# All 22 hidden chunks of the FFNs' up projection in seven products, opened by the two products that need only the first token half

## The chip, the cores and the metric

The kernel runs on one core of a Trainium2 chip. The metric is the device time of one execution in microseconds (us); before is the kernel as it was, after is the kernel with the change. One execution of each is also recorded by the hardware profiler, and the views below are of that record. PE is TensorE, DVE is VectorE, ACT is ScalarE, POOL is GpSimd and SP is SyncE, which only issues loads here.

## What is computed

A trunk of two layers on 768 tokens (a prompt of 512 and a sample of 256, which share the weights). Each layer is a macaron block:

```
x = x + 0.5 * swiglu_ffn(rmsnorm(x, norm_g[li, 0]), ffn_w1[li, 0], ffn_w2[li, 0])
x = x + mixer(rmsnorm(x, norm_g[li, 1]))        # layer 0: HGRN2, layer 1: windowed attention
x = x + 0.5 * swiglu_ffn(rmsnorm(x, norm_g[li, 2]), ffn_w1[li, 1], ffn_w2[li, 1])

def swiglu_ffn(x, w1, w2):
    gate, up = jnp.split(x @ w1, 2, axis=-1)
    return (jax.nn.silu(gate) * up) @ w2
```

The width is 1024 and the FFN's hidden width is 2816, all in fp32. There are four FFNs: f0, then HGRN2, f1 and f2 one behind the other, then the attention, f3.

## The kernel before

**Numbers.** Every fp32 factor is split into a high part (a cast on ACT) and a low part (a subtraction on DVE or, for one weight block in seven, on POOL), and each product is three matmuls: high by high, high by low, low by high. An operand is ready when both parts are: the split of a token tile is L266 (ACT) and L267 (DVE), that of a weight L199 and L200, or L166 and L167 for a weight that is staged whole.

**Chunks and halves.** The hidden width is 22 chunks of 128; chunk i has 128 gate columns and 128 up columns of w1. The tokens are two halves of 384 (three blocks of 128 each), the model width two parts of 512. The normed and transposed input of an FFN thus has four tiles, b00 and b10 (first half of tokens, parts 0 and 1) and b01 and b11 (second half). Each tile has four slices of 128, held in two pairs `kp`.

**Plain and in seven products.** Chunks 0 and 1 are multiplied plainly (`up_plain`): for each token half, gate and up are 8 slices x 3 matmuls of 128x384 each, so 96 matmuls for a chunk and 192 for the two. Chunks 2 to 21 go by `up_pair`, a Strassen-Winograd scheme over (gate, up) x (token half) with seven products p1 to p7 of 12 matmuls each, 84 for a chunk. A product takes one combination of weight blocks, which is staged, and one factor of the tokens:

```
FACTOR = {"p1": "b00", "p2": "b10", "p3": "b11", "p4": "t4", "p5": "t1", "p6": "t2", "p7": "t3"}
```

The sums t1 to t4 combine the four tiles. `sums` and `mix` make them once for an FFN, on DVE (L350, L351, L353, L354), each followed by a split (a cast on ACT, L266, and a subtraction on DVE, L267), for each of two halves kp of a part. `product` issues the 12 matmuls of a product (L421). The hidden values of four chunks (a group) go through `down_quad`, also in seven products (L479), with `add_x` adding the results to x (L501).

**Weights.** SP loads raw columns into four buffers `wr` and, for the chunks in seven products, one more block into `s3`. POOL's accumulating DMAs (L141) add a11 to the block in s3 and a22 to a21, in place. DVE adds a11 += a21 (L206) and a12 += a11 (L210) between the splits. `quad_steps` lists the staging of one chunk's seven weights in the order UP; `plain_steps` stages a whole 128-column block. Staging runs ahead of use as far as eight staged buffers `w` allow.

**Order.** The code is written in program order, and a scheduler places each instruction in the queue of its engine; each engine works through its queue in order and waits by semaphores. What is to be mixed into the opening of an FFN (the transposes of the second token half, the sums) is put on a list of deferred steps, which `run_later` takes from. Before an FFN the residual additions of the stage ahead end block by block, and each block of 128 tokens is normed at once (`norm_block`: L303 and L304 on ACT, L305 and L306 on DVE), transposed on PE (L323), scaled on its way out of PSUM by ACT (L326), and split.

## Time and profile before

| what | value |
|---|---|
| time, median of 3 runs | 2863.37 us (2861.89 to 2866.12) |
| time of the profiled execution | 2862.54 us |
| its span, first to last instruction | 2860.7 us |
| mean granted clock of TensorE | 0.995 |
| busy share of PE, DVE, ACT, POOL | 98%, 77%, 46%, 11% |
| first matmul of the opening of f1, and of its down projection | 1070.57 us, 1136.32 us |
| first matmul of the down projection of f2, of f3 | 1635.36 us, 2422.50 us |

Rows in order of time give the start from the beginning of the span, how long the row was busy, engine, source line and operation, the program's names for the output and inputs, the shapes, the number of instructions that the row holds, and in square brackets how long the engine was idle before it and what released it. L261, L262 and L263 are the three matmuls of a plain product, L421 those in the seven products. In the page's groups the numbers behind the shapes are total busy us, mean ns of one, and idle time ahead with its releaser. A matmul's duration contains waiting in a pipeline; the distance from one start to the next is what it costs.

### The profile page before, as it was taken

To read this page: it belongs to the slowest core of one execution; us is meant where nothing else is said; L and a number is where in the kernel's file an instruction comes from. 1 tells how busy PE (TensorE), PEld (TensorE's weight loads), DVE (VectorE), ACT (ScalarE), POOL (GpSimd) and SP (SyncE) were. 2 spreads that over 40 slices of the span, in tenths; PEclk is the share of its full clock that TensorE was granted. 3 is DMA by queue.
4 is the path that set the end of the run, shared out by engine and by line. 5 is a ranking of instruction groups with operands and counts; after the bars stand their busy time and mean duration, and the time that the engine had idled before them with its cause. 6 is when DMAs were issued, how large, how long until landed. Compare 5 with 4: busy or idle time off the path is not lost. (4 is left out here: it accounts for less than half of the span.)

```text
span 2860.7 us, 40520 instructions
## 1 busy us (share of the span) xinstructions
PE 2802.9 (98%) x15225; PEld 2559.9 (89%) x15225; DVE 2195.0 (77%) x3846; ACT 1318.2 (46%) x2454; POOL 303.9 (11%) x306
## 2 busy tenths in 40 slices
PE   8999999999999999999999999999999899999998
PEld 8899999889899889998998999989887779989897
DVE  7788787477577658778878878887859978778877
ACT  7344443434344435433444543444457755434443
POOL 1111111000000001111111111111000001111110
PEclk9999999999999999999999999999999999999999
DMA  6555454311111133554544355544412113554442
GB/s 165 128 122 124 120 133 118 111 45 38 45 41 34 64 92 89 133 132 119 122 118 107 92 137 129 124 118 120 131 54 74 45 37 91 134 129 123 118 122 96
DMA packets 330101, 291.37 MB, mean 102 GB/s; under 512 B 11608, under 2 KB 257840, under 8 KB 329904
## 3 DMA queue, kind: packets, MB, share of 16 engines
q1 hardware_dynamic: 294064, 212.43, 25.0%
q0 software_dynamic: 31680, 62.93, 12.7%
q10 hardware_dynamic: 4160, 13.42, 1.3%
q8 instruction: 119, 1.95, 0.3%
q14 instruction: 78, 0.64, 0.1%
HBM read 216.39 MB, written 9.44 MB: 79 GB/s over the span
## 5 line engine op out<-in xcount | busy, mean ns | idle before, releaser
L421 PE MATMUL ps<-big,w 128*128 128x384 f32 x6720 | 1172.6, 334 | 3.3 <-DVE tA L444 2.9
L421 PEld LDWEIGHTS ps<-big,w 128*128 128x128 f32 x6720 | 1165.6, 188 | 8.6 <-DVE tA L444 6.9
L199 ACT CAST w<-wr 128x512 fp32r<-128x512 f32 x600 | 416.1, 707 | 724.6 <-PE ps L421 328.3
L479 PE MATMUL ps<-w,big 128*128 128x512 f32 x2520 | 586.8, 391 | 15.8 <-DVE x L501 15.6
L479 PEld LDWEIGHTS ps<-w,big 128*128 128x128 f32 x2520 | 469.6, 188 | 127.9 <-DVE x L501 16.7
L200 DVE TENSOR_TENSOR w<-wr,w 128x512 fp32r<-128x512 f32 (+1 forms) x520 | 437.0, 850 | 95.4 <-ACT w L199 86.5
L501 DVE SCALAR_TENSOR_TENSOR x<-ps,x 128x512 f32<-128x512 f32 x468 | 305.5, 682 | 21.5 <-PE ps L479 11.1
L141 POOL DMA_DIRECT2D s<-wr x120 | 105.6, 880 | 1620.4 <-DMA wr<-in_ffn_w_dram 611.5
L261 PE MATMUL ps<-w,big 128*128 128x512 f32 x624 | 249.5, 400 | 0.2
L263 PE MATMUL ps<-w,big 128*128 128x512 f32 x624 | 245.5, 394 | 2.0 <-DVE big L330 1.4
L262 PE MATMUL ps<-w,big 128*128 128x512 f32 x624 | 244.8, 392 | 0.0
L266 ACT CAST big<-tA 128x384 fp32r<-128x384 f32 x296 | 147.9, 512 | 171.2 <-DVE tA L449 70.4
L261 PE MATMUL ps<-big,w 128*128 128x384 f32 (+2 forms) x640 | 221.0, 347 | 3.4 <-ACT big L266 2.0
L262 PE MATMUL ps<-big,w 128*128 128x384 f32 (+2 forms) x640 | 217.1, 339 | 0.7 <-DVE big L267 0.4
L263 PE MATMUL ps<-big,w 128*128 128x384 f32 (+2 forms) x640 | 215.7, 337 | 0.0
L167 DVE TENSOR_TENSOR w<-wr,w 128x1024 fp32r<-128x1024 f32 x92 | 111.3, 1220 | 81.7 <-ACT w L166 57.6
L267 DVE TENSOR_TENSOR big<-tA,big 128x384 fp32r<-128x384 f32 x296 | 164.1, 565 | 8.4 <-ACT big L266 5.1
L206 DVE TENSOR_TENSOR wr<-wr,wr 128x512 f32<-128x512 f32 (+1 forms) x100 | 79.3, 793 | 113.4 <-DMA wr<-wr 84.6
L141 POOL DMA_DIRECT2D wr<-wr x100 | 87.2, 872 | 678.2 <-DVE tA L350 332.6
L166 ACT CAST w<-wr 128x1024 fp32r<-128x1024 f32 x92 | 96.6, 1052 | 121.7 <-PE ps L262 100.5
L263 PEld LDWEIGHTS ps<-w,big 128*128 128x128 f32 x624 | 117.6, 188 | 28.1 <-DVE big L330 2.1
L261 PEld LDWEIGHTS ps<-w,big 128*128 128x128 f32 x624 | 118.0, 189 | 22.5 <-ACT w L166 0.3
(170 smaller groups left out, 3298.6 us busy)
## 6 DMA issues: line engine op xcount, KB each, us to landing
wr<-in_ffn_w_dram SPq DMA_DIRECT2D x264, 512.0 KB, 3.8
s<-in_ffn_w_dram SPq DMA_DIRECT2D x120, 256.0 KB, 3.0
s<-wr POOLq DMA_DIRECT2D x120, 256.0 KB, 3.8
wr<-wr POOLq DMA_DIRECT2D x80, 256.0 KB, 3.8
wr<-in_hg_w_in_dram SPq DMA_DIRECT2D x40, 512.0 KB, 3.7
wr<-wr POOLq DMA_DIRECT2D x20, 512.0 KB, 4.6
spill<-x ACTq DMA_DIRECT2D x12, 512.0 KB, 3.2
x<-spill ACTq DMA_DIRECT2D x12, 512.0 KB, 3.2
```

Of the source, the lines that this page charges most:

```text
L141: self.nc.gpsimd.dma_start(out, src, accum_op=ALU.add)
L167: self.nc.vector.tensor_sub(lo, raw, hi.bitcast(F32))
L199: nc.scalar.copy(h, src)
L200: (eng or nc.vector).tensor_sub(l, src, h.bitcast(F32))
L261: nc.tensor.matmul(out, a[0], b[0], start=first, stop=False)
L262: nc.tensor.matmul(out, a[0], b[1], start=False, stop=False)
L263: nc.tensor.matmul(out, a[1], b[0], start=False, stop=last)
L266: self.nc.scalar.copy(hi, src)
L267: self.nc.vector.tensor_sub(lo, src, hi.bitcast(F32))
L421: self.nc.tensor.matmul(ps, a[x], b[y], start=first and k == 0 and i == 0, stop=k == 3 and i == 2, skip_group_check=True,)
L479: nc.tensor.matmul(ps, a[x], w[y], start=name == chain and kp == 0 and q == 0, stop=kp == 1 and q == 2, skip_group_check=True,)
L501: self.nc.vector.scalar_tensor_tensor(x, ps, c, x, ALU.mult, ALU.add)
```

## The change

`up_plain` and PLAIN are gone, and all 22 chunks are planned in seven products. In the first group of an FFN `open_pairs` runs ahead: for chunks 0 and 1, then for 2 and 3, the products p1 (with b00) and p2 (with b10), both of which have gate columns as weight, 96 matmuls in all. Their weights are the two halves of the gate columns, which are staged whole by the plain step; so the gate columns of these four chunks are loaded twice, once there and once for the rest. `up_pair` then does the other five products of these chunks, in the order REST. `quad_steps` does a11 += a21 after p7 and a12 += a11 after p4 in that order. `mix` puts t3 ahead of t1, and the b01 tile, which no product uses by itself, is no longer split.

```
-PLAIN = 2
-GROUPS = (NF - PLAIN) // 4
+GROUPS = NF // 4
+REST = ("p7", "p5", "p4", "p6", "p3")
...
-        def p1():
-            split("p1", [a11])
-            nc.vector.tensor_add(a11, a11, a21)
-
-        def p2():
-            split("p2", [a12])
-            nc.vector.tensor_add(a12, a12, a11)
...
+        own = {"p1": [a11], "p2": [a12], "p3": [a12], "p4": [a22], "p5": [a21], "p6": [a11], "p7": s3}
+        second = lambda: nc.vector.tensor_add(a11, a11, a21)
+        fourth = lambda: nc.vector.tensor_add(a12, a12, a11)
+        after = {"p7": second, "p4": fourth} if order == REST else {"p1": second, "p2": fourth}
...
             for kp in range(2):
-                self.put(f"b{part}{half}", kp, self.tn[(part, half)][:, kp])
+                if part or not half:
+                    self.put(f"b{part}{half}", kp, self.tn[(part, half)][:, kp])
...
         sub(b22, b12, b22)
         sub(b12, b11, b12)
+        put("t3", b22)
         put("t1", b12)
         sub(b11, b11, b22)
         sub(b21, b21, b11)
         put("t4", b21)
-        put("t3", b22)
         put("t2", b11)
...
+            self.plan_quad((tag, i), (gate, up), (NC, P), REST if i < 4 else UP)
+
+        for i in range(4):
+            self.plan((tag, i, "gate"), w1[:, i * P : (i + 1) * P], (NC, P))
...
+    def open_pairs(self, tag, js):
+        opened = {j: (self.ps(H), self.tmp(H)) for j in js}
+        for part in range(2):
+            for j, (a, v) in opened.items():
+                key = (tag, j, "gate")
+                w = tuple(t[:, 4 * part : 4 * part + 4, :] for t in self.take(key))
+                self.multiply(a, w, FACTOR["p2" if part else "p1"], not part, part)
+                if part:
+                    self.done(key)
+                    self.nc.scalar.activation(a, a, AF.Silu)
+                else:
+                    self.nc.scalar.copy(v, a)
+                if part or js[0] or len(self.deferred) > 3:
+                    self.run_later()
+        return opened
...
             if g == 0:
-                ts = {}
-                for half in range(2):
-                    for j in range(PLAIN):
-                        t = ts[2 * j + half] = self.up_plain(tag, j, half)
-                        name = f"b{j}{half}"
-                        if name != "b01":
-                            put(name, t, 0)
-                gather(ts, 0)
+                for i in range(0, 4, 2):
+                    opened.update(self.open_pairs(tag, (i, i + 1)))
                 self.run_later(len(self.deferred))
```

Line numbers shift with it: L398 of after is a matmul of any product (before L421), L259 and L260 the split of a token tile (before L266 and L267), L205 and L206 the additions a11 += a21 and a12 += a11 (before L206 and L210), L474 a matmul of the down projection (before L479).

How the instructions stand now is shown at three places of f1's opening. Names in front of the underscore are the program's tiles. First PE, behind the matmuls that need only the first token half. Before, the second half of the two plain chunks follows, on the split b01 tile (big_1284):

```order
3676 L261 MATMUL ps_1304_9214<-big_1276_9044,w_1263_9001 128x384
3677 L262 MATMUL ps_1304_9214<-big_1276_9044,w_1263_9001 128x384
3678 L263 MATMUL ps_1304_9214<-big_1276_9044,w_1264_9002 128x384
3679 L261 MATMUL ps_1307_9245<-big_1284_9103,w_1231_8834 128x384
3680 L262 MATMUL ps_1307_9245<-big_1284_9103,w_1231_8834 128x384
```

After, at the end of the opening products (big_1288 is a part of b10), come products on the sums: big_1313 and big_1317 are the two halves of t3, big_1314 and big_1318 those of t1, big_1316 one of t2:

```order
3542 L398 MATMUL ps_1311_9191<-big_1288_9068,w_1276_9026 128x384
3543 L398 MATMUL ps_1329_9300<-big_1313_9208,w_1293_9113 128x384 x6
3544 L398 MATMUL ps_1330_9301<-big_1314_9211,w_1294_9117 128x384 x6
3545 L398 MATMUL ps_1328_9299<-big_1316_9219,w_1301_9158 128x384
3546 L398 MATMUL ps_1343_9402<-big_1313_9208,w_1325_9274 128x384 x2
3547 L398 MATMUL ps_1329_9300<-big_1317_9224,w_1293_9113 128x384
3548 L398 MATMUL ps_1330_9301<-big_1318_9227,w_1294_9117 128x384
```

So the products that use the sums have moved up to directly behind the work on the first token half.

Second ACT, between b10 and the casts of b11 (before: big_1280 is b01, big_1287 is b11):

```order
790 L326 ACTIVATE big_1280_9086<-ps_1279_9082,cols_92 128x384
791 L326 ACTIVATE big_1280_9086<-ps_1281_9088,cols_92 128x384
792 L326 ACTIVATE big_1280_9086<-ps_1282_9093,cols_92 128x384
793 L326 ACTIVATE big_1280_9086<-ps_1283_9098,cols_92 128x384
794 L266 CAST big_1284_9103<-big_1280_9086 128x2x384
795 L266 CAST big_1285_9106<-big_1280_9086 128x2x384
796 L326 ACTIVATE big_1287_9125<-ps_1286_9121,cols_92 128x384
797 L326 ACTIVATE big_1287_9125<-ps_1288_9127,cols_92 128x384
798 L326 ACTIVATE big_1287_9125<-ps_1289_9132,cols_92 128x384
799 L326 ACTIVATE big_1287_9125<-ps_1290_9137,cols_92 128x384
800 L266 CAST big_1291_9142<-big_1287_9125 128x2x384
801 L266 CAST big_1292_9145<-big_1287_9125 128x2x384
```

After (big_1296 is b01, big_1303 is b11; two copies L418 stand ahead of b01's four):

```order
801 L319 ACTIVATE big_1296_9125<-ps_1299_9137,cols_92 128x384
802 L199 CAST w_1293_9113<-s3_1249_8876 128x512
803 L199 CAST w_1294_9117<-wr_1248_8874 128x512
804 L416 ACT_TABLE_LOAD
805 L416 ACTIVATE ps_1289_9071<-ps_1289_9071 128x384
806 L199 CAST w_1300_9154<-wr_1248_8874 128x512
807 L199 CAST w_1301_9158<-wr_1247_8872 128x512
808 L416 ACTIVATE ps_1291_9073<-ps_1291_9073 128x384
809 L319 ACTIVATE big_1303_9166<-ps_1302_9162,cols_92 128x384
810 L319 ACTIVATE big_1303_9166<-ps_1304_9168,cols_92 128x384
811 L319 ACTIVATE big_1303_9166<-ps_1305_9173,cols_92 128x384
```

The b01 casts are gone, and four staging casts, a table load and two Silus stand between b01 and b11.

Third DVE, at the residual additions ahead of f1's opening (x_1193 before and x_1205 after are token block 2). Before:

```order
1155 L499 TENSOR_TENSOR x_1193_8537<-ps_1244_8897,x_1193_8537 128x512
1156 L305 RECIPROCAL stat_1246_8912<-stat_1246_8912 128x1
1157 L306 TENSOR_SCALAR big_1245_8911<-x_1193_8537,stat_1246_8912 128x1024
1158 L499 TENSOR_TENSOR x_1194_8539<-ps_1247_8917,x_1194_8539 128x512
1159 L465 TENSOR_TENSOR x_1191_8533<-x_1191_8533,x_1194_8539 128x512
```

After, wr_1247 and wr_1248 being the raw gate and up columns of chunk 0:

```order
1172 L494 TENSOR_TENSOR x_1205_8561<-ps_1256_8921,x_1205_8561 128x512
1173 L205 TENSOR_TENSOR wr_1247_8872<-wr_1247_8872,wr_1248_8874 128x512
1174 L206 TENSOR_TENSOR wr_1247_8872<-wr_1247_8872 128x512
1175 L298 RECIPROCAL stat_1258_8936<-stat_1258_8936 128x1
1176 L299 TENSOR_SCALAR big_1257_8935<-x_1205_8561,stat_1258_8936 128x1024
1177 L494 TENSOR_TENSOR x_1206_8563<-ps_1259_8941,x_1206_8563 128x512
```

The two additions of the weight staging now stand between block 2's residual addition and its norm. In f2 the first of them stands behind block 1's residual additions.

More of the change, by code (lines that the diff above doesn't have):

```diff
@@ L396, in plan_ffn, with multiply @@
             self.plan((tag, "last", c), w2[(NF - 2) * P :, c * 512 : (c + 1) * 512], (2, 512))
-    def up_plain(self, tag, j, half):
-        pss = []
-        for c in range(2):
-            wh, wl = self.take((tag, j, c))
-            ps = self.ps(H)
-            for k in range(NC):
-                b = self.operand(f"b{k // 4}{half}", k % 4)
-                self.mm3(ps, (wh[:, k, :], wl[:, k, :]), b, k == 0, k == NC - 1)
-                if half == 0 and k in (((), (2, 6)), ((3, 7), (3, 7)))[j][c]:
-                    self.run_later()
-            if half:
-                self.done((tag, j, c))
-            pss.append(ps)
-        t = self.tmp(H)
-        self.nc.scalar.activation(t, pss[0], AF.Silu)
-        self.nc.vector.tensor_mul(t, t, pss[1])
-        return t
     def product(self, key, name, src, ps, first, last):
-        wh, wl = self.take((*key, name))
+        self.multiply(ps, self.take((*key, name)), src, first, last)
+        self.done((*key, name))
+    def multiply(self, ps, w, src, first, last):
         for k in range(4):
-            a, b = (wh[:, k, :], wl[:, k, :]), self.operand(src, k)
+            a, b = (w[0][:, k, :], w[1][:, k, :]), self.operand(src, k)
             for i, (x, y) in enumerate(((0, 0), (0, 1), (1, 0))):
```

44 lines of the change are left out of this document (18 added, 26 removed).

## The prediction

> **What bounds the kernel now.** I read the page's busy times first, then TensorE (PE) in order of time at one opening of an FFN, and there the queues of ScalarE (ACT), VectorE (DVE) and GpSimd (POOL). The second FFN (f1) stands for the others.
>
> ```profile
> PE 2802.9 (98%) x15225; PEld 2559.9 (89%) x15225; DVE 2195.0 (77%) x3846; ACT 1318.2 (46%) x2454; POOL 303.9 (11%) x306
> ```
>
> PE is busy for 98% of the span, so a removed matmul is worth its pitch if its successors are ready. Any new wait of PE is paid in full.
>
> ```profile
> 1070.57 0.60 PE L261 MATMUL ps<-big,w 128*128 128x384 f32 x2
> ...
> 1084.66 0.33 PE L263 MATMUL ps<-big,w 128*128 128x384 f32 x1
> ...
> 1089.00 0.33 PE L261 MATMUL ps<-big,w 128*128 128x384 f32 x1
> ...
> 1107.20 1.03 PE L421 MATMUL ps<-big,w 128*128 128x384 f32 x5
> ...
> 1136.32 2.01 PE L479 MATMUL ps<-w,big 128*128 128x512 f32 x8
> ```
>
> These are f1's first plain matmul (1070.57), two rows 25 matmuls apart, the first matmul of a product (1107.20) and the first of the down projection (1136.32). The pitch is 4.34 / 25 = 0.1736 us. The 192 plain matmuls take 33.33 of the 36.63 us before 1107.20; the other 3.30 are transposes of the second half and short waits.
>
> **Matmuls removed.** Four chunks cost 2 x 96 + 2 x 84 = 360 matmuls before and 4 x 84 = 336 after. That is 24 x 0.1736 = 4.17 us for an FFN, 16.7 for four, and the whole gain; the built program's order has these 96 fewer on PE.
>
> **The cover that goes with them.** Before, 192 matmuls need no sum of token halves; after, only the 96 of the two opening products do not. PE ends those at 1070.57 + 16.67 + 3.30 = 1090.54. Next in its queue stand 60 matmuls (10.42 us) that use all eight sum operands (t3, t1, t4, t2, two halves each). When are these ready?
>
> ```profile
> 1075.72 1.59 ACT L266 CAST big<-big 128x768 fp32r<-128x768 f32 x2
> 1077.18 2.03 ACT L326 ACTIVATE big<-ps,cols 128x384 f32<-128x384 f32 x4
> 1079.04 1.62 ACT L266 CAST big<-big 128x768 fp32r<-128x768 f32 x2
> 1080.50 2.11 ACT L326 ACTIVATE big<-ps,cols 128x384 f32<-128x384 f32 x4
> 1082.50 1.56 ACT L266 CAST big<-big 128x768 fp32r<-128x768 f32 x2
> 1084.09 1.28 ACT L412 ACT_TABLE_LOAD   x1
> ```
>
> ```profile
> 1083.37 1.83 DVE L267 TENSOR_TENSOR big<-big,big 128x768 fp32r<-128x768 f32 x2 [1.58 <-ACT big L266]
> 1085.11 0.95 DVE L350 TENSOR_TENSOR big<-big,big 128x768 f32<-128x768 f32 x1
> ...
> 1089.74 0.95 DVE L354 TENSOR_TENSOR big<-big,big 128x768 f32<-128x768 f32 x1
> 1090.61 0.95 DVE L350 TENSOR_TENSOR big<-big,big 128x768 f32<-128x768 f32 x1
> ...
> 1095.41 0.68 DVE L200 TENSOR_TENSOR w<-wr,w 128x512 fp32r<-128x512 f32 x1
> 1096.02 0.95 DVE L353 TENSOR_TENSOR big<-big,big 128x768 f32<-128x768 f32 x1
> ...
> 1099.83 2.69 DVE L267 TENSOR_TENSOR big<-big,big 128x768 fp32r<-128x768 f32 x3
> ```
>
> ```profile
> 1070.00:1085.00 15.00, 14.91 (x96) 14.27 (x95) 11.83 (x15) 14.98 (x26) 1.73 (x2) 1.00 0.44 105
> 1085.00:1100.00 15.00, 15.00 (x88) 15.00 (x88) 14.88 (x21) 8.37 (x14) 0.00 (x0) 1.00 0.01 2
> 1107.00:1136.00 29.00, 29.00 (x170) 29.00 (x169) 22.22 (x34) 14.37 (x25) 3.97 (x4) 1.00 0.50 119
> ```
>
> ACT turns out b10, b01 and b11 without a gap, and DVE's chain of sums starts when b11 is split. The table of stretches (columns PE, weight loads, DVE, ACT, POOL, clock, share of the DMA engines, GB/s) says that ACT is the limit up to 1085 (14.98 of 15) and DVE after it (14.88 of 15). Before, the last operand is out at 1099.83 + 3 x 0.87 = 1102.4, 4.8 us ahead of PE. The change takes 16.67 us of cover from that. What it does to the chain is priced from these rows:
>
> ```profile
> L199 ACT CAST w<-wr 128x512 fp32r<-128x512 f32 x480 | 289.7, 620 | 565.3 <-PE ps L421 254.2 <-PE ps L479 251.0 <-issue 38.5
> L442 ACT ACTIVATE ps<-ps 128x384 f32<-128x384 f32 x80 | 37.9, 474 | 14.5 <-PE ps L421 14.5
> L438 ACT COPY tA<-ps 128x384 f32<-128x384 f32 x80 | 37.9, 473 | 3.0 <-PE ps L421 1.3
> L206 DVE TENSOR_TENSOR wr<-wr,wr 128x512 f32<-128x512 f32 x80 | 54.8, 685 | 0.6
> L210 DVE TENSOR_TENSOR wr<-wr 128x512 f32<-128x512 f32 x80 | 56.7, 709 | 1.2
> 1102.59 2.15 POOL L200 TENSOR_TENSOR w<-wr,w 128x512 fp32r<-128x512 f32 x1 [21.05 <-ACT w L199]
> 1103.97 1.32 DVE L210 TENSOR_TENSOR wr<-wr 128x512 f32<-128x512 f32 x1
> ```
>
> ACT, between the casts of b10 and those of b11: the b01 casts go (1080.50 - 1079.04 = 1.46). Two copies (0.95), four staging casts (4 x 0.62 = 2.48), the table load (1.28) and two Silus (0.95) come, 5.66 in duration. Neighbours overlap by about 0.1 us each, so 4.9, and net +3.4. The load moves from behind the b11 casts to ahead of them. The first sum then starts at 1085.11 + 3.4 = 1088.5.
>
> DVE: eight sums and eight splits of a pitch of 0.87 (1090.61 - 1089.74), 13.9 us, and four staging subtractions among them at 0.61 (1096.02 - 1095.41), 2.4 us. The last operand is out at 1104.8. The plain product's L413 and its split, which stood among the sums before, are gone; the b01 split went from an idle stretch and gives nothing. A staging subtraction of POOL also falls into the chain; beside such a one the a12 addition took 1.32 us instead of 0.71, so +0.6 at most here. Six matmuls (1.04) follow the last operand, so PE ends the 60 at 1105.9 to 1106.5 instead of 1090.54 + 10.42 = 1100.96. I take a wait of 5.0 us, the end without POOL's delay; bounds 4.0 (a third of ACT's additions lie in gaps) and 5.6.
>
> The Trainium skill ("SBUF — State Buffer", section "SBUF: two separate sides") calls the port pair of DVE and GpSimd an exclusive lock, for which the loser waits out the whole instruction. By it the added delay could be as long as POOL's 2.15 us, and the total 1.5 us higher for each FFN than by the 0.6 of the row; the measured row decides.
>
> The rest of the opening is PE's: 180 matmuls, 31.2 us or 15 products. From 1107 to 1136 DVE spent 22.22 us on 14 products, so 15 need some 24 of 31. POOL and SP each issue 24 instructions more, since chunks 0 to 3 load their gate twice; DMA shares of 0.44, 0.01 and 0.50 hide that, for nothing.
>
> **A new wait ahead of the opening.** DVE's queue of after has quad 0's a11 addition right behind the residual addition of token block 2. It waits for POOL's accumulating DMA. Queued behind it are that block's norm and the second half's additions; ACT, PE's transposes and so the first matmul wait for these.
>
> ```profile
> 1060.40 0.68 DVE L499 TENSOR_TENSOR x<-ps,x 128x512 f32<-128x512 f32 x1
> 1062.63 0.16 DVE L305 RECIPROCAL stat<-stat 128x1 f32<-128x1 f32 x1 [1.55 <-ACT stat L304]
> ...
> 1060.19 0.88 POOL L141 DMA_DIRECT2D wr<-wr  x1 [2.29 <-DVE stat L305]
> ...
> wr<-wr POOLq DMA_DIRECT2D x1, 256.0 KB, 3.3
> ...
> 1555.31 1.88 DVE L501 SCALAR_TENSOR_TENSOR x<-ps,x 128x512 f32<-128x512 f32 x3
> 1558.32 0.69 DVE L501 SCALAR_TENSOR_TENSOR x<-ps,x 128x512 f32<-128x512 f32 x1 [1.13 <-PE ps L263]
> ...
> 1557.83 0.86 POOL L141 DMA_DIRECT2D wr<-wr  x1 [4.61 <-DVE x L501]
> ```
>
> In f1 the DMA is issued at 1060.19 and lands 3.3 later, 1063.5. The addition and the next one (0.6 each at their pitch) put the norm at 1064.7 instead of 1062.63: 2.1 us late, of which I take 1.8, as PE has a little other work. Bounds are 0 (issued early enough) and 2.1. In f2 it stands behind block 1's additions, which end at 1557.2, and the DMA lands at 1561.1: 4.0 late, taken as 3.4 since down matmuls remain; bounds 1.0 and 4.5. The fourth FFN follows a projection as f1 does: 1.8. The first has no additions ahead of it: 0.
>
> **Sum**, against the profiled execution (2862.54, span 2860.7): f0 -4.17 + 5.0 = +0.8; f1 -4.17 + 5.0 + 1.8 = +2.6; f2 -4.17 + 5.0 + 3.4 = +4.2; f3 +2.6. Together +10.2, so 2872.7; the median of the runs (2863.37) is 0.83 above this execution, which gives 2873.6.
>
> **The rivals.** *The operands come in time, faster.* Place: the second halves of t4 and t2. Price: up to 16.7 us. It decides where the last operand is out by 1100, that is 5 us earlier than I count. ACT's 8.37 busy of 15 after 1085 and its casts that wait for staging slots rather than for work speak for it; DVE's 14.88 of 15 speaks against it. With the early waits small too the time is 2847 to 2857, about 2852.
>
> *Waits eat just the saving.* With 4.0 us of wait and half the early shifts (0, 0.9, 1.7, 0.9) the sum is -0.7 + 3.5 = +2.8, 2866; with none, 2863. Measurement of this kernel tells from no change about 0.2%, 5.7 us, so this is 2857.6 to 2869.1.
>
> *The clock falls, much slower.* The sums' waits could halve the clock:
>
> ```profile
> 2313.68 0.50 PE L1157 MATMUL ps<-tA,big 128*128 128x512 f32 x1 [0.79 <-DVE tA L267]
> 2315.94 1.94 PE L1144 MATMUL ps<-ident_r,big 128*128 128x128 f32 x8 [1.75 <-DVE big L1138]
> ...
> 2316.00:2323.00 7.00, 6.54 (x20) 5.19 (x21) 3.30 (x8) 1.18 (x3) 0.00 (x0) 0.53 0.27 80
> ```
>
> Waits of 0.79 and 1.75 us with one matmul between were followed by 7 us at 0.53: 7 x 0.47 = 3.3 us lost. At two to four openings that is +7 to +13, 2880 to 2887. Against it: the 5 us here are spread over 60 matmuls, mostly below 0.9 us at once.
>
> The Trainium skill ("TensorE: Matmul & The Clock Gate", section "Why this matters for your kernels") warns of idle gaps above some 3 us only. By that rule no opening loses clock and 2873.6 stands; the row above shows the loss behind shorter gaps, so this rival keeps a chance.
>
> That PE's work does not shrink is excluded by the order, and has none.
>
> **How the numbers follow.** The forecast case (waits of 4 to 5.6 us, early shifts as counted) gets 0.45 and 2869 to 2880; the clock 0.15; waits that eat the saving 0.22; operands in time 0.18. The faster case and the slower ones give faster 0.18, same 0.22, slower 0.60. The range leaves out the deeper half of the faster case and a tenth above: 2855 to 2886.
>
> **What would show it.** The multiply line should have matmuls with idle time behind DVE's splits of t4 and t2 in all four openings, 4 to 5.6 us in each; the first sum of f1 should start some 18 us after the opening's first matmul (before 14.54) with ACT full until then; DVE should show the a11 addition waiting for a DMA ahead of f1, f2 and f3. Wrong it would be if the sums start within 16 us, if PE runs through the 60 matmuls without a gap, or if the waits last over 8 us since two chunks' banks, freed by DVE behind the sums, come late as well.

## The result

| | median | range | runs |
|---|---|---|---|
| before | 2864.56 us | 2861.89 to 2866.12 | 5 |
| after | 2907.15 us | 2896.0 to 2910.24 | 5 |

The ratio is 1.0143 (95% interval 1.0133 to 1.0154), so after is slower by 42.6 us. The prediction was 2873.6 us within 2855 to 2886: the sign is right, the size is four times what was forecast. The profiled execution of after has a span of 2905.3 us against 2860.7, 44.6 more.

### The profile page after: what moved, and what is told of

The parts are those of the page before. It is cut to its first block, busy times and chain, and to the rows that moved or that the text cites. A ratio compares the mean times of both kernels' runs of the same rounds, so it can differ in the third digit from the quotient of the medians.

```text
span 2905.3 us, 40580 instructions
## 1 busy us (share of the span) xinstructions
PE 2808.2 (97%) x15129; PEld 2552.1 (88%) x15129; DVE 2230.3 (77%) x3910; ACT 1331.6 (46%) x2484; POOL 372.7 (13%) x330
## 5 line engine op out<-in xcount | busy, mean ns | idle before, releaser
L398 PE MATMUL ps<-big,w 128*128 128x384 f32 x7392 | 1315.0, 337 | 44.2 <-DVE tA L442 17.3
L398 PEld LDWEIGHTS ps<-big,w 128*128 128x128 f32 x7392 | 1291.7, 189 | 63.8 <-DVE tA L442 18.5
L199 ACT CAST w<-wr 128x512 fp32r<-128x512 f32 (+1 forms) x616 | 425.5, 704 | 739.7 <-PE ps L398 330.7
L474 PE MATMUL ps<-w,big 128*128 128x512 f32 x2520 | 586.5, 391 | 16.9 <-DVE x L496 16.7
L474 PEld LDWEIGHTS ps<-w,big 128*128 128x128 f32 x2520 | 469.6, 188 | 128.7 <-DVE x L496 19.3
L141 POOL DMA_DIRECT2D s<-wr x128 | 112.9, 882 | 1643.2 <-DMA wr<-in_ffn_w_dram 961.0
L259 ACT CAST big<-tA 128x384 fp32r<-128x384 f32 x296 | 149.2, 513 | 182.5 <-DVE tA L444 89.9
L205 DVE TENSOR_TENSOR wr<-wr,wr 128x512 f32<-128x512 f32 (+1 forms) x108 | 85.0, 787 | 140.0 <-DMA wr<-wr 102.1
L200 POOL TENSOR_TENSOR w<-wr,w 128x512 fp32r<-128x512 f32 x88 | 173.9, 1976 | 115.7 <-ACT w L199 110.6
L141 POOL DMA_DIRECT2D wr<-wr x108 | 95.3, 883 | 679.0 <-DVE tA L344 269.1
L260 DVE TENSOR_TENSOR big<-tA,big 128x384 fp32r<-128x384 f32 x296 | 165.1, 565 | 6.0 <-ACT big L259 4.9
L256 PEld LDWEIGHTS ps<-w,big 128*128 128x128 f32 x624 | 117.4, 188 | 28.4 <-DVE big L323 2.0
L254 PEld LDWEIGHTS ps<-w,big 128*128 128x128 f32 x624 | 117.7, 189 | 22.3 <-issue 0.6
L255 PEld LDWEIGHTS ps<-w,big 128*128 128x128 f32 x624 | 117.8, 189 | 22.3
L254 PE MATMUL ps<-big,w 128*128 128x512 f32 (+1 forms) x384 | 133.9, 349 | 0.0
```

Of the source, the lines that this page charges most:

```text
L141: self.nc.gpsimd.dma_start(out, src, accum_op=ALU.add)
L199: nc.scalar.copy(h, src)
L200: (eng or nc.vector).tensor_sub(l, src, h.bitcast(F32))
L254: nc.tensor.matmul(out, a[0], b[0], start=first, stop=False)
L255: nc.tensor.matmul(out, a[0], b[1], start=False, stop=False)
L256: nc.tensor.matmul(out, a[1], b[0], start=False, stop=last)
```

## The profile after

First the busy times on the page and, from the view by lines, the group of the products' matmuls (the page's rows: count, total busy us, mean ns, idle us ahead with its releasers), of after and then of before.

```profile
PE 2808.2 (97%) x15129; PEld 2552.1 (88%) x15129; DVE 2230.3 (77%) x3910; ACT 1331.6 (46%) x2484; POOL 372.7 (13%) x330
```
```profile
L398 PE MATMUL ps<-big,w 128*128 128x384 f32 x7392 | 1315.0, 337 | 44.2 <-DVE tA L442 17.3 <-ACT big L259 9.8 <-DVE tA L439 4.4
```
```profile
L421 PE MATMUL ps<-big,w 128*128 128x384 f32 x6720 | 1172.6, 334 | 3.3 <-DVE tA L444 2.9
```

PE has the 96 fewer instructions that were counted (15225 - 15129), yet its products wait 44.2 us instead of 3.3. The sums account for some of that (L259 is the cast of a token tile). The largest part has another releaser, L442: the subtraction `v -= b` in `up_pair`, which reads a product from PSUM and frees its bank. No term of the prediction's sum stands for it.

To see where in the openings the time lies, I count the starts of their 128x384 matmuls, from the first to the first matmul of the down projection, in us. The stretches end at the start of the 96th and of the 156th matmul, so a wait counts to the matmuls behind it, and the last stretch has 181 steps:

| opening | before, all | after, all | first 96 matmuls | next 60 | last 180 |
|---|---|---|---|---|---|
| f0 | 69.85 | 80.98 | 26.56 (before 23.07) | 14.63 | 39.79 |
| f1 | 65.75 | 73.76 | 22.05 (19.81) | 16.07 | 35.64 |
| f2 | 65.80 | 75.21 | 22.04 (19.86) | 14.24 | 38.93 |
| f3 | 65.93 | 76.70 | 22.06 (19.99) | 14.38 | 40.26 |
| without a gap | | | | 10.42 | 31.42 |

The openings are 39.3 us longer in all: the first 96 matmuls cost 10.0 more than before, the 60 behind the sums 17.7 more than their pitch, the last 180 another 28.9 more, less 16.7 for the removed matmuls and 0.6 for what before waited there. The other 5.3 lie outside the openings. The last 180 were put down as running free.

Here they are in f3, PE in order of time.

```profile
2407.16 1.15 PE L398 MATMUL ps<-big,w 128*128 128x384 f32 x5 [1.08 <-ACT tA L418]
...
2420.87 7.28 PE L398 MATMUL ps<-big,w 128*128 128x384 f32 x40 [0.22 <-ACT tA L434]
2433.54 2.93 PE L398 MATMUL ps<-big,w 128*128 128x384 f32 x8 [5.39 <-DVE tA L442]
```

PE catches up with the sums, runs 40 matmuls, and then stops for 5.39 us until DVE has done L442. DVE's own queue at that time:

```profile
2425.19 0.55 DVE L439 TENSOR_TENSOR tA<-tA,ps 128x384 f32<-128x384 f32 x1
2425.66 1.32 DVE L200 TENSOR_TENSOR w<-s,w 128x512 fp32r<-128x512 f32 x1
2432.33 0.69 DVE L205 TENSOR_TENSOR wr<-wr,wr 128x512 f32<-128x512 f32 x1 [5.35 <-DMA wr<-wr]
2432.94 0.55 DVE L442 TENSOR_TENSOR tA<-tA,ps 128x384 f32<-128x384 f32 x1
```

L442 stands one place behind the staging addition a11 += a21 (L205) of a later chunk, which waits 5.35 us for POOL's accumulating DMA. POOL, in all four openings (the fourth row is f3, and the last is its DMA issue):

```profile
43.71 13.09 POOL L200 TENSOR_TENSOR w<-wr,w 128x512 fp32r<-128x512 f32 x1 [0.40 <-ACT w L199]
...
1104.31 11.21 POOL L200 TENSOR_TENSOR w<-wr,w 128x512 fp32r<-128x512 f32 x1 [1.35 <-ACT w L199]
...
1612.42 13.53 POOL L200 TENSOR_TENSOR w<-wr,w 128x512 fp32r<-128x512 f32 x1 [1.29 <-ACT w L199]
...
2412.88 13.54 POOL L200 TENSOR_TENSOR w<-wr,w 128x512 fp32r<-128x512 f32 x1 [1.45 <-ACT w L199]
2426.38 0.86 POOL L141 DMA_DIRECT2D wr<-wr  x1
```

One staging subtraction of POOL takes 11.2 to 13.5 us where one like it, outside such a stretch, takes 1.63:

```profile
2400.42 1.63 POOL L200 TENSOR_TENSOR w<-wr,w 128x512 fp32r<-128x512 f32 x1
```

It begins among the sums and ends about when they do. Up to L439 DVE runs sums, splits and staging subtractions back to back, all with two inputs in SBUF (its busy time from 2411 to 2426 is shown at the clock, further below). In f3 POOL's instruction ends 1.2 us after the start of L439, the first one with an input in PSUM. In f1, where it is the shortest (11.21, up to 1115.52), it ends behind a gap in DVE's run:

```profile
1114.69 2.52 DVE L260 TENSOR_TENSOR big<-big,big 128x768 fp32r<-128x768 f32 x2 [0.32 <-ACT big L259]
```

Only behind POOL's subtraction is the DMA of the third quad issued, and it takes longer than usual, beside three loads of SP (view of DMA issues, 2426 to 2433; KB of each, last column us from issue to landing):

```profile
wr<-wr POOLq DMA_DIRECT2D x1, 256.0 KB, 5.9
wr<-in_ffn_w_dram SPq DMA_DIRECT2D x2, 512.0 KB, 5.8
s<-in_ffn_w_dram SPq DMA_DIRECT2D x1, 256.0 KB, 7.1
```

Alone it took 3.3 before. Last, the table of stretches (start and end, length, then PE, weight loads, DVE, ACT, POOL, clock, DMA share, GB/s):

```profile
2426.00:2433.00 7.00, 2.15 (x13) 1.83 (x11) 1.65 (x3) 0.63 (x2) 1.25 (x2) 0.96 0.76 190
2433.00:2440.00 7.00, 6.46 (x22) 6.46 (x23) 6.47 (x13) 2.96 (x6) 3.01 (x3) 0.55 0.76 174
...
64.00:71.00 7.00, 7.00 (x33) 7.00 (x34) 7.00 (x11) 2.77 (x6) 3.01 (x3) 0.78 0.61 146
...
1122.00:1129.00 7.00, 6.68 (x37) 6.38 (x38) 6.94 (x13) 3.38 (x7) 2.86 (x3) 1.00 0.79 179
...
1633.00:1640.00 7.00, 7.00 (x29) 7.00 (x30) 6.41 (x11) 2.93 (x6) 2.89 (x4) 0.70 0.75 163
```

The first two rows are f3. Behind the wait PE is busy again, but at a granted clock of 0.55: 7 x 0.45 = 3.15 us lost on top. The other three rows lie behind the waits of f0, f1 and f2, which were 5.03, 1.64 and 5.21 us: 1.5, 0 and 2.1 us of clock. So the waits for L442 are 17.3 and the clock behind them 6.8 of the 28.9.

## The experiments

The runs carry the numbers E1 to E17; they are told by subject. My theory A: DVE's unbroken run keeps POOL out, POOL's late DMA holds DVE, and DVE holds PE's bank. Rival B: DVE simply has too much work around the sums, and POOL's long row is only a symptom. Ratios are against before, run on the same chip beside each kernel, with 95% intervals.

**E1. POOL's subtraction goes to DVE.**

```
-            split(name, own[name], nc.gpsimd if up and name == "p5" else None)
+            split(name, own[name], nc.gpsimd if up and name == "p5" and order != REST else None)
```

> Edit: in the chunks that are opened (0 to 3 of each FFN) the low part of the p5 weights is subtracted on DVE instead of POOL; DVE's order is otherwise the same row for row. Theory A: after's long wait of PE (5.2, 1.8, 5.4 and 5.6 us in f0 to f3) is released by DVE's v -= b (L442), which stands behind a11 += a21 of the third quad (L205), which waits 5.35 us for POOL's accumulating DMA, and that DMA stands in POOL's queue behind one subtraction of 128x512 that lasts 11.2 to 13.5 us because DVE's unbroken run of sums keeps it from its operands. Then with the subtraction gone from POOL the DMA is issued some 10 us earlier, L205 waits under 1 us, PE's wait at L442 falls to under 1.5 us in every opening, the half clock behind it goes too, and the time falls by 18 to 26 us, to 2881 to 2889; two more 0.6 us operations on DVE are already in that. Rival B, banks: the four opened chunks hold four of the eight PSUM banks, and PE would wait for v -= b in any case since DVE does the sums first: the wait of 5 us stays and the time is within 5 us of after (2902 to 2912).

Measured 2882.9, ratio 1.0107 (1.0089 to 1.0124); before took 2853.05 on that chip, so the ratio has to be compared and not the time. The wait at `v -= b` is gone, as A says. DVE's addition does not wait any more (its row in f3 first). But the gain, 1.0107 against 1.0143 to 1.0147, is about 10 us and not 18 or more: PE now waits at L439 and for the splits.

```profile
2411.58 0.68 DVE L205 TENSOR_TENSOR wr<-wr,wr 128x512 f32<-128x512 f32 x1
```
```profile
L398 PE MATMUL ps<-big,w 128*128 128x384 f32 x7392 | 1308.9, 336 | 36.5 <-DVE tA L439 10.3 <-ACT big L259 9.1 <-DVE big L260 7.3
```

**E2 and E3. The additions in place stand directly ahead of the split that needs them**, alone (E2) and with E1's edit (E3).

```
+        before = {"p6": second, "p3": fourth} if order == REST else {}
...
+            if name in before:
+                before[name]()
```

> Edit: in the opened chunks a11 += a21 is done just ahead of the split for p6, and a12 += a11 just ahead of that for p3, instead of right behind p7 and p4; POOL keeps its subtraction. In DVE's queue v -= b of chunk 0 then stands ahead of the third quad's a11 += a21. Theory A: POOL's subtraction still lasts over 10 us and the accumulating DMA is still late, but DVE's wait for it no longer stands ahead of v -= b, so that PE's wait there falls from 5.4 to under 2 us and the time falls by 12 to 25 us, to 2882 to 2895. Rival B, banks: no change of the wait, 2902 to 2912. A third way, that the late weights of chunk 2 only move the wait to p7 of chunk 2: a wait of 3 to 5 us some 60 matmuls later, and 2895 to 2907.

> Edit: both of the former, the p5 subtraction on DVE and the additions late. Theory A: nothing is left for the second edit to win behind the first, so the time is that of the first alone within 3 us, 2879 to 2889, and still above before (2864), because the wait for the sums (3.8 to 5.7 us over the 60 matmuls behind the opening) and the 2.2 us that the first 96 matmuls of each opening take longer than before are untouched. Rival: the two waits are independent, then the gains add up and the time is below 2875.

E2: 2897.42, 1.0152 (1.0136 to 1.0167): a miss. The late DMA no longer holds DVE, but it holds ACT: the copy L438 of a product from PSUM (`w = c`, L434 of after) stands behind casts of the late weight, and PE waits 12.3 us for it.

```profile
L402 PE MATMUL ps<-big,w 128*128 128x384 f32 x7392 | 1312.8, 337 | 42.6 <-ACT tA L438 12.3 <-ACT big L263 9.5 <-DVE tA L443 8.5
```

E3: 2883.63, 1.0105 (1.0086 to 1.0124), the same as E1. So what counts is that the DMA is late, more than which queue waits for it.

**E4. E3, and the Silus of the opened chunks behind p7's copy.**

```
-                    self.nc.scalar.activation(a, a, AF.Silu)
...
+        nc.scalar.activation(a, a, AF.Silu)
```

> Edit: both of the former, and the four Silus of the opening with their table load are done in up_pair behind the copy of p7 instead of in the opening, so that in ACT's queue they stand behind the casts of b11. The working of the prediction has them (2.2 us of ACT) ahead of b11's casts and so ahead of the sums. If ACT's queue sets the start of the sums, then the first sum starts 1.5 to 2.5 us earlier from the opening's first matmul, the second-token waits of the sums and of the copies shrink by as much, and the time is 6 to 10 us below the run without this edit, 2871 to 2881. Rival: the sums start with what DVE does before (it waits for the second quad's DMA ahead of b11's split), then the time is within 3 us of the run without the edit.

2879.52, 1.0091 (1.0076 to 1.0106): 4.1 us less than E3, with intervals that overlap, where 6 to 10 were expected. The trace speaks for the rival. In f3 (first matmul at 2369.62) ACT's casts of b11 start after 13.85 us instead of 15.92 in E3, yet the first sum, L348 here, starts after 19.99 us against 20.35. Ahead of the split of b11 DVE has waited 3.97 us in front of the second quad's a11 addition; in f1 and f2 it is the same (4.23 and 2.88 us).

```profile
2383.47 1.56 ACT L263 CAST big<-big 128x768 fp32r<-128x768 f32 x2
```
```profile
2385.33 0.69 DVE L205 TENSOR_TENSOR wr<-wr,wr 128x512 f32<-128x512 f32 x1 [3.97 <-issue]
...
2389.61 1.82 DVE L348 TENSOR_TENSOR big<-big,big 128x768 f32<-128x768 f32 x2
```

**After once more, on the chip of E5 to E7.**

> The changed kernel as it is, so that it and the edits below are measured beside the same runs of the kernel before. Its ratio to before was 1.0143; expected again 1.013 to 1.016. In its trace POOL's one subtraction among the sums should again last 11 to 14 us in each opening, and the p1 copies of chunks 2 and 3 should again hold PE for 1.2 us (before the 73rd matmul of the opening).

2905.54, 1.0147 (1.013 to 1.0164), which repeats the result.

**E6. E1, and the copies of the opening products on DVE instead of ACT.**

```
-                    self.nc.scalar.copy(v, a)
+                    self.nc.vector.tensor_copy(v, a)
```

> Edit: p5 subtraction of the opened chunks on DVE (as in the first experiment), and in the opening the copy of p1 from PSUM is made by DVE instead of ACT. PE may not add p2 to a bank before p1 has been copied from it, and ACT makes these copies behind the casts of b11. If that is why the first 96 matmuls take 22.05 us instead of 19.9, then the waits of 0.3 to 0.45 and 1.25 us in front of p2 go (DVE has idle time there, waiting for the second quad's DMA) and the first 96 take 20 to 20.8 us; the time falls by 3 to 7 us below the first experiment, ratio 1.0085 to 1.0100. Rival: DVE stands in its wait for the second quad's DMA when the copy is due, PE waits for DVE as long as it did for ACT, and the time is that of the first experiment (1.0107) or more.

2908.3, 1.0158 (1.0143 to 1.0173): the copies came to stand behind DVE's own wait for a DMA, and the first 96 matmuls of f1 to f3 took 25.7 to 27.9 us.

**E5. E4, with the second half transposed and summed for one kp after the other.**

```
+        for kp in range(2):
+            steps.append(lambda kp=kp: self.turn_pair(kp, row))
+            steps.append(lambda kp=kp: self.sums(kp))
```

> Edit: on top of the late Silus (1.0091), the second token half is transposed and scaled in the order kp 0 of both parts, then kp 1 of both, and the sums of kp 0 stand in front of the second. The prediction's step says that the sums' chain on DVE (16 operations of 0.87 us) sets the wait of the 60 matmuls behind the opening, and that ACT's work on b01 and b11 sets its start. Then the chain starts some 2 us earlier and the four openings win 1.5 to 2.5 us each: ratio 1.005 to 1.0075. Rival: the chain only gains an idle stretch in its middle (kp 1 is not there yet) and the end stays, ratio 1.008 to 1.010.

2887.32, 1.0081 (1.0066 to 1.0096), no gain over E4 (1.0091) that the intervals show.

**E7. Cover given back: chunk 0 is plain again, chunks 1 to 3 are opened** (on E3).

```
-                for i in range(0, 4, 2):
-                    opened.update(self.open_pairs(tag, (i, i + 1)))
+                plain = [self.up_plain(tag, 0)]
+                put("b00", plain[0], 0)
+                for js in ((1, 2), (3,)):
+                    opened.update(self.open_pairs(tag, js))
+                plain.append(self.up_plain(tag, 1))
```

> Edit: chunk 0 is plain again (both token halves, b01 split again), chunks 1 to 3 are opened with p1 and p2 and go on in seven products, p5 subtraction on DVE, additions late. 348 matmuls of the opening stand against 360 before and 336 after: 12 x 0.1736 = 2.08 us less than before per FFN, 8.3 us in four, 0.29%. The cover ahead of the first sum product is 48 + 72 + 48 = 168 matmuls (29.2 us) instead of 96 (16.7). If the lost cover is what made after slower, then the sums are there in time (before they were 4.8 us early with 192) and the ratio is 0.996 to 0.999, faster than before. Rival: any opening by p1 and p2 costs more in copies, Silus and doubled gate loads than it saves, ratio above 1.001.

2873.92, 1.0034 (1.0022 to 1.0046), above the 0.996 to 0.999 that were expected. 168 matmuls need no sum (two halves of 48 plain ones and 72 of the opened chunks) where after has 96, and the waits behind the sums are gone. What is left is the late third quad, on ACT: in f1 its cast waits for the DMA, and the copy behind it holds PE.

```profile
1118.65 1.14 ACT L199 CAST w<-wr 128x512 fp32r<-128x512 f32 x2 [4.23 <-DMA wr<-wr]
```

**E11. The direct test of A: in after, two reciprocals of 128x1 on DVE in each opening**, one behind each kp's sums, with a result that nothing reads.

```
             self.mix(*tiles, lambda name, src: self.put(name, kp, src))
+            self.nc.vector.reciprocal(self.stat(1), self.tn[(1, 0)][:, kp, 0, :1])
```

> Edit: the changed kernel with one more DVE instruction in each half of the sums, a reciprocal of one column (128x1, one input, its result is not used), in the middle of the run of two-input operations; everything else stands as in after, POOL keeps its subtraction of the p5 weights. Theory A (DVE's unbroken run of operations with two inputs in SBUF keeps POOL's subtraction out, and that it is out makes the rest late): POOL's subtraction ends at the reciprocal, in 2 to 6 us instead of 11 to 13.5, the DMA behind it is issued 7 to 10 us earlier, PE's wait at v -= b falls below 2 us, and the time falls by 10 to 20 us in spite of two instructions more, ratio 1.008 to 1.011 instead of 1.0147. Rival: POOL's subtraction is long for another reason (its own speed beside DMAs, the length of DVE's queue): it stays at 11 us or more and so does the time, within 0.1%.

2892.3, 1.0106 (1.0091 to 1.0122): two more instructions make the kernel some 12 us faster. DVE, then POOL and PE of f3:

```profile
2406.31 0.15 DVE L357 RECIPROCAL stat<-big 128x1 f32<-128x1 f32 x1
...
2418.49 0.68 DVE L205 TENSOR_TENSOR wr<-wr,wr 128x512 f32<-128x512 f32 x1
```
```profile
2403.97 3.56 POOL L200 TENSOR_TENSOR w<-wr,w 128x512 fp32r<-128x512 f32 x1 [1.13 <-ACT w L199]
2412.59 0.88 POOL L141 DMA_DIRECT2D wr<-wr  x1 [5.06 <-DVE big L348]
```
```profile
2412.98 17.27 PE L399 MATMUL ps<-big,w 128*128 128x384 f32 x97 [0.20 <-ACT tA L435]
```

POOL's subtraction takes 3.56 us instead of 13.54, the DMA goes out ahead of DVE's need, the addition does not wait, and PE runs 97 matmuls where it stopped after 40. Counted from f3's first matmul, the DMA goes out after 32.2 us instead of 37.2. That is 5.0 us sooner and not 10, as POOL, now free, still waits 5.06 us until DVE has done L348. The last 180 matmuls of the four openings are now 7.7 us over their pitch instead of 28.9. So A's chain is shown, and B, which has no gain from more work on DVE, falls. The 60 matmuls ahead became longer, 24.6 over instead of 17.7. Most of the growth, 4.3 us, lies in f2, where the granted clock was 0.50 for 10.2 us; beside the sums of f2 in after it stayed at 1.00. What started that, I did not settle.

```profile
1609.60:1619.80 10.20, 9.12 (x26) 7.88 (x27) 10.20 (x14) 4.04 (x6) 3.63 (x2) 0.50 0.30 71
```

**E8 to E10. Variants of E7**: p4 ahead of p5 in the order of the opened chunks (the diff, with the same step in `up_pair`); the opened chunks ahead of the plain one; both.

```
-REST = ("p7", "p5", "p4", "p6", "p3")
+REST = ("p7", "p4", "p5", "p6", "p3")
```

> Edit: on the kernel with one plain chunk (1.0034), the order of the opened chunks is p7, p4, p5, p6, p3 instead of p7, p5, p4, p6, p3. What is left there is one wait of 2.6 to 4.4 us in each opening before p4 of chunk 2 or 3, released by ACT's copy of p7, which stands in ACT's queue behind casts that wait 4.2 us for the third quad's accumulating DMA; p4's weights need no accumulation, p5's do. If that order is what puts the late weights ahead of the copy, the wait shrinks to under 1.5 us and the ratio falls to 0.998 to 1.001. Rival: the copy stays behind another cast that waits for the same DMA (that of p7's block), and the ratio stays at 1.002 to 1.004.

> Edit: on the kernel with one plain chunk, the opened products of chunks 1 to 3 stand ahead of the plain chunk's first half. Their gate weights come free 48 matmuls (8.3 us) earlier, so the rest of these chunks is staged earlier and the third quad's raw columns are loaded earlier. If the late third quad is a matter of staging space, the wait of 2.6 to 4.4 us goes and the ratio is 0.997 to 1.000. Rival: the four buffers that the plain chunk holds are the limit, they are freed at the same time as before, and the ratio stays at 1.002 to 1.005.

> Edit: both of the former two. If either cause holds the ratio is that of the better one or up to 0.001 lower; if neither, 1.002 to 1.005.

1.0059 (1.0044 to 1.0074), 1.0071 (1.0055 to 1.0088) and 1.0068 (1.0053 to 1.0083), all above E7's 1.0034, while each edit was expected to bring it down; only E8's interval still touches E7's. Their causes I did not follow up.

**E12 to E14. Fewer opened chunks than in E7**: chunks 1 and 2, chunk 1 alone (the diff), and chunks 1 and 2 with the additions where after has them; the rest go as chunks 4 to 21 do.

```
-                for js in ((1, 2), (3,)):
+                for js in ((1,),):
```

> Edit: as the kernel with one plain chunk (1.0034), but only chunks 1 and 2 are opened; chunk 3 goes in the usual order, its gate columns are loaded once. The matmul count is the same (348 in an opening, 2.08 us less than before), the cover ahead of the first sum product is 144 matmuls (25.0 us). Theory: the wait of 2.6 to 4.4 us that was left there comes from staging (three gate blocks and the plain chunk fill the staged buffers, so the third quad is loaded late); with one gate block less it shrinks to under 1.5 us, and the sums still come in time, since the last operand is not due before 5 to 8 us behind the cover: ratio 0.997 to 1.000. Rival: the cover of 168 was needed, the sums are late by 2 to 4 us, ratio 1.002 to 1.006.

> Edit: the same with only chunk 1 opened; cover 120 matmuls (20.8 us). Theory staging: no late quad any more, but the sums are now late by 1 to 4 us: ratio 0.999 to 1.004. If the lost cover counts for less than I think, it is at or below the run with two opened, 0.996 to 0.999.

> Edit: as with two opened chunks, but a11 += a21 and a12 += a11 stand behind p7 and p4 as in the changed kernel. Theory staging: where DVE meets the third quad's late DMA does not matter while that DMA is in time: within 0.1% of the run with two opened. Rival: the place of the additions decides which queue is held up, and it differs by more than 0.15% either way.

1.0088 (1.0074 to 1.0102), 1.0046 (1.0034 to 1.0059) and 1.0088 (1.0074 to 1.0102). E12 is above both its theory (0.997 to 1.000) and its rival (1.002 to 1.006), so a lack of staging space, as it was told there, is not shown to be the cause; E14 says that the place of the additions does not matter there. In E13, with one opened chunk, the openings of f1 to f3 are down to 66.2 to 66.5 us, 0.3 to 0.7 above before; the loss has moved to f0's opening (81.34) and to late starts.

**E15 and E16. The early wait: in after, and in E13, DVE's a11 addition is held behind the last norm of the block.**

```
+            with self.tc.issue_after(self.normed) if order == REST else nullcontext():
+                nc.vector.tensor_add(a11, a11, a21)
```

> Edit: the changed kernel with a11 += a21 of the opened chunks placed behind the last norm of the token blocks in DVE's queue; nothing else. The prediction's early wait (that addition ahead of a norm, waiting for a DMA) was summed at 7 us over f1 to f3; after's openings started 2.3 and 2.6 us late in f2 and f3 and not at all in f1. If that addition is the reason, f2 and f3 start as early as before relative to the stage ahead and the time falls by 3 to 6 us: ratio 1.0125 to 1.0137 beside 1.0147. Rival: the late starts come from something else, and the ratio stays at 1.0143 to 1.0155.

> Edit: the kernel with one plain chunk and only chunk 1 opened (1.0046), with a11 += a21 behind the last norm. There PE waited some 10 us in all for norms and the splits behind them ahead of f1 to f3, and lost only 4.8 us inside an opening (before: 0.8 to 1.0). If the early addition is the reason for the first, the ratio falls by 0.003 to 0.004, to 1.0005 to 1.002; it is still not below 1, since 8.3 us of saved matmuls stand against some 15 us of waits inside the openings. A ratio below 1 would say that one chunk fewer in plain products can pay.

E15: 2895.82, 1.013 (1.0112 to 1.0148), less than after's 1.0147, but the intervals overlap. In its trace f1 to f3 start 0.3, 3.6 and 6.2 us sooner behind the down projection ahead of them than in after. E16: 2861.37, 0.9998 (0.999 to 1.0007), 10.8 us below E13 and equal to before. From one down projection's first matmul to the next opening's first, f1 to f3 gain 2.0, 4.9 and 1.6 us against E13: in these two traces the early wait costs 8.5 us. PE's group of products has 9.2 us of idle time left.

```profile
L407 PE MATMUL ps<-big,w 128*128 128x384 f32 x7056 | 1239.2, 335 | 9.2 <-ACT big L266 4.4 <-DVE big L267 2.2 <-DVE tA L466 1.7
```

**E17. E16, with f0 opened by two plain chunks as before**, since f0's opening is still 79.7 us in E16 and 69.85 before.

```
+    def plain(self, tag):
+        return 2 if tag == "f0" else 1
```

> Edit: as the kernel with one plain chunk and one opened chunk, additions behind the norms (0.9998), but the first FFN opens as before with two plain chunks; three FFNs save 12 matmuls each (6.2 us in all). In that kernel f0's opening lost 16.9 us against 5.0 before, f1 to f3 only 3.5 to 4.2 in a longer stretch. If f0 alone ate the saving, the time falls by about 12 - 2.1 = 10 us: ratio 0.9955 to 0.9975, faster than both. Rival: what f0 loses is made up elsewhere (its loads come early and only shift), ratio 0.9985 to 1.0005.

2854.79 (2851.91 to 2859.7 in 11 runs) against 2861.05, 0.9981 (0.9972 to 0.999). It is faster than both kernels, by 6 us. That is just at the 0.2% which a measurement can tell and less than expected. The gain is as large as the pitch of the 36 removed matmuls, 36 x 0.1736 = 6.2 us, but the trace does not show it there: the openings of f1 to f3 took 65.55, 65.43 and 65.70 us, only 0.2, 0.4 and 0.2 less than before, so waits ate most of what was removed, and f0's took 71.62, 1.8 more. The span is 5.5 us shorter than in the trace of before, all of it outside the openings, where the two traces differ in their clock too. Where the 6 us come from is not shown.

```profile
L409 PE MATMUL ps<-big,w 128*128 128x384 f32 x6972 | 1219.9, 335 | 4.2 <-DVE tA L471 3.1 <-ACT big L266 0.9
```

## Why the prediction was right and wrong

**Matmuls removed, -16.7: right.** The order and the page's count agree.

**The wait for the sums, +20.0: right in sum, in part by luck.** The 60 matmuls took 4.2, 5.65, 3.8 and 4.0 us over their pitch, 17.7 in all, within the bounds of 4.0 to 5.6 but for a little at both ends. Two errors cancel in that: in f1 to f3 PE ends the first 96 matmuls after 22.2 us instead of 19.97, and the first sum starts after 19.6, 18.9 and 19.06 us instead of 17.9. Nor does ACT set that start, as the prediction says. In f3 (first matmul at 2389.22):

```profile
2405.15 1.59 ACT L259 CAST big<-big 128x768 fp32r<-128x768 f32 x2
2406.60 0.89 ACT L418 COPY tA<-ps 128x384 f32<-128x384 f32 x2
```
```profile
2404.00 0.69 DVE L205 TENSOR_TENSOR wr<-wr,wr 128x512 f32<-128x512 f32 x1 [3.64 <-DMA wr<-wr]
...
2406.54 1.82 DVE L260 TENSOR_TENSOR big<-big,big 128x768 fp32r<-128x768 f32 x2
2408.28 1.82 DVE L344 TENSOR_TENSOR big<-big,big 128x768 f32<-128x768 f32 x2
```

DVE comes to the split of b11 (L260) and to the first sum (L344) without having been idle for ACT. What holds it is the second quad's a11 addition, which waits 3.64 us for a DMA (4.17 in f1, 3.50 in f2); the sum of the prediction has nothing for this wait. E4 had ACT's casts 2.1 us earlier, and the sums of f1 to f3 did not follow. Only in f0 does DVE wait for ACT there, 0.26 us.

**The first 96 matmuls, 0: wrong, 10.0.** p2 adds to the bank in which p1 lies, so p2 of a chunk can't begin until ACT has copied p1 out. For chunks 2 and 3 these copies (L418 above) stand behind the casts of b11, and PE waits 1.08 us for them in the first row of f3 shown above. I counted the copies as load on ACT and not as something PE waits for. These waits are 3.8 us of the 10.0 in the whole run; in f0 another 2.10 are a wait for ACT's scaling of the second half (L319). The rest I have not traced.

**The 180 matmuls behind, 0: the step that failed, 28.9.** "The rest of the opening is PE's" was argued from DVE's share of busy time (24 of 31), which does not see one instruction that waits at the head of a queue. The cause was named at the end, "two chunks' banks, freed by DVE behind the sums, come late as well", and given neither a price nor a chance. Its root is in the sentence on POOL: "so +0.6 at most here" took the delay that POOL causes DVE. What happens is the reverse. DVE's sums keep POOL out for the length of their run, and what stands behind that subtraction in POOL's queue is a DMA that DVE itself needs at the end of that same run. E11 shows the links; it and E1 price the chain at 10 to 12 us net, since part of what is won is waited for elsewhere.

The Trainium skill ("SBUF — State Buffer", section "SBUF: two separate sides") says that whichever of the two starts first has the pair for its whole instruction. These traces show more than that: POOL lost to some 15 instructions of DVE in a row, 13.54 us. I read the rule for one instruction each, and in one direction.

**The clock.** As a rival it had 0.15 and was told of the sums' waits. It came, by 6.8 us, behind the bank's waits, which were not in the forecast. Beside the sums it came in two openings only. In f0 and f1 it was 0.50 and 0.51 for 3.4 us, behind waits of 1.52 and 1.31 us; in f2 and f3 it stayed at 1.00 behind waits of 1.32 and 1.33 us. The last row is f3:

```profile
46.60:50.00 3.40, 3.36 (x11) 2.76 (x10) 3.40 (x5) 0.88 (x2) 3.40 (x1) 0.50 0.52 154
1108.10:1111.50 3.40, 3.36 (x11) 2.78 (x10) 3.40 (x5) 0.85 (x2) 3.40 (x1) 0.51 0.53 159
...
2411.00:2426.00 15.00, 12.65 (x65) 10.73 (x64) 15.00 (x20) 9.46 (x16) 13.55 (x2) 1.00 0.28 71
```

**The early wait, +7.0: right in kind.** From one down projection's first matmul to the opening's, f1 starts 1.7 us sooner than before, f2 1.8 and f3 3.9 later, 4.0 in sum. DVE's waits are there:

```profile
1071.86 0.69 DVE L205 TENSOR_TENSOR wr<-wr,wr 128x512 f32<-128x512 f32 x1 [2.33 <-issue]
...
1577.65 0.69 DVE L205 TENSOR_TENSOR wr<-wr,wr 128x512 f32<-128x512 f32 x1 [3.44 <-issue]
...
2380.81 0.69 DVE L205 TENSOR_TENSOR wr<-wr,wr 128x512 f32<-128x512 f32 x1 [2.08 <-issue]
```

The rows name no releaser, but POOL's DMA for the same block goes out 3.4, 3.5 and 3.4 us before each addition and takes 3.3 us to land. In f2 and f3 they reach PE; in f1 the start is not late, which the count of 1.8 missed.

**The doubled gate loads, 0:** by bytes they are hidden. But POOL's DMA is 5.9 us instead of 3.3 beside SP's loads, and 2.6 us of that lie on the chain above. That these loads fall there is a part of the chain too: in all four openings the first of them goes out 0.07 us behind POOL's DMA, and the profile names POOL's subtraction as what released it. In E11 the DMA took 4.3.

**The sum.** -16.7 + 10.0 + 17.7 + 28.9 - 0.6 + 5.3 = 44.6. With 0 for the last 180 it would have been 15.7; the forecast was 10.2.

What stays open: which property of DVE's instruction lets POOL in (the reciprocal has one input and is short), why the 60 matmuls got longer in E11, and where E17's 6 us come from.

## What to carry to other kernels

Before a change takes the cover away from a chain on one engine, list for every queue what stands directly behind an instruction that waits, and which of these frees a buffer or a PSUM bank; the wait of the chain itself may be the smaller part. A share of busy time says nothing on that. Where DVE runs long stretches on SBUF alone, keep POOL's instructions, and DMA issues that stand behind them in its queue, out of these stretches, or break the stretch. And give up only as much cover as the chain behind leaves: the kernel with one plain chunk instead of two in three FFNs (E17) was 6 us faster than before, the one with none in all four 42.6 slower.

## What the runs showed of the hardware

- A 128x512 subtraction of POOL with SBUF inputs took 11.2 to 13.5 us while DVE ran two-input instructions on SBUF back to back, and 1.63 outside. One DVE instruction of 0.15 us in the run brought it to 2.8 to 3.6.
- Waits of 5.03, 5.21 and 5.39 us on PE were followed by 7 us at a clock of 0.78, 0.70 and 0.55; one of 1.64 us by a full clock. Waits of 1.31 and 1.52 us were followed by 3.4 us at 0.51 and 0.50 in two places, waits of 1.32 and 1.33 us by a full clock in two others.
- POOL's accumulating DMA of 256 KB took 5.9 us beside two loads of 512 KB each and one of 256 KB, and 3.3 without.
